# Token-major weight chunks of 512 columns in the mixers, the mLSTM gate taken before its transposes, four heads rotated at a time

## The chip, the cores and the metric

The kernel runs on one core of one Trainium2 chip. The metric is the device time of one execution in microseconds; lower is better. Five engines work side by side: PE (TensorE, matrix products), ACT (ScalarE), DVE (VectorE), POOL (GpSimd, hardly used here) and SP, which issues the transfers from memory. Each runs its own queue in order and waits for the others on semaphores.

## The reference

256 tokens of width 1024 pass through two blocks, all in float32. The change touches the two mixers of the first block: an mLSTM, and a causal attention with shared keys and values.

```python
def mlstm_mixer(x, norm_g, w_in, b_gates, h_norm_g, w_out):
    u = rmsnorm(x, norm_g) @ w_in
    q, k, v, o, gi, gf = jnp.split(u, M_SPLITS, axis=-1)   # 4 heads: q, k of 128, v, o of 256 each
    ...
    h = mlstm_chunkwise(q, k, v, i_pre, f_pre)
    h = rmsnorm(h, h_norm_g.reshape(M_HEADS, M_DV)).reshape(b_, s_, M_HEADS * M_DV)
    h = h * jax.nn.sigmoid(o.astype(jnp.float32))
    return h.astype(x.dtype) @ w_out

def shared_kv(x, norm_g, w_kv, k_norm_g, cos, sin):
    kv = rmsnorm(x, norm_g) @ w_kv
    k, v = jnp.split(kv, 2, axis=-1)                       # 8 heads of 128
    k = apply_partial_rope(rmsnorm(k.reshape(b_, s_, A_HEADS, A_DH), k_norm_g), cos, sin)
    ...

def moba_mixer(x, norm_g, w_q, q_norm_g, w_o, kb, vb, kmean, cos, sin):
    q = (rmsnorm(x, norm_g) @ w_q).reshape(b_, s_, A_HEADS, A_DH)
    q = apply_partial_rope(rmsnorm(q, q_norm_g), cos, sin) * (A_DH ** -0.5)
    ...                                                    # 256 tokens: causal softmax(q k) v
    return o @ w_o
```

After each mixer stands a convolutional feed-forward (width 2816), then the second block: two layers with a 31-tap convolution branch, an attention over the 64 best keys, and a gated output projection.

## The kernel before

Every large product is made exact enough in float32 by a split: `split_w` and `split_x` cut an operand into a high and a low part of 12 significant bits each (ACT copies the high part, DVE subtracts to get the low one), and `mm3` (lines 569 to 571) issues three matmuls, high*high, high*low, low*high. A matmul has 128 rows of contraction, 128 stationary columns and up to 512 moving columns.

**Two orientations.** `gemm_fm` (and `gemm_pair`, two of them into one PSUM bank) has the weights stationary and the 256 tokens moving, so features come out on partitions. `gemm_tm` has 128 tokens stationary and the weights moving, so a half of the tokens comes out on partitions, as wide as the weight chunk. Of the mixers' projections, before the change, `a_w_v`, `w_k`, `b_w_q` and `w_v` are token-major from chunks of 256 columns, two halves of the tokens in one bank; `a_w_o` is feature-major. All have eight contraction blocks, so a chunk of 256 costs 2 x 8 x 3 = 48 matmuls of 256 moving columns.

**mLSTM.** The gates' sums run through a small chain: a transpose of `a_s` to four rows, a copy and a running maximum on DVE (`scan`, line 477), a transpose back, then the masks E. Behind the heads' outputs `hn` (token-major) come the four `a_w_o` chunks: a `gemm_pair`, four transposes of `hn` into `tp`, then for each 128 features `so = product * r` (DVE), tanh (ACT), `y = (so + 1) * tp` (DVE), and the split of `y` with the norm's gain into `ys`, on which `proj_res("a_w_out")` works.

**Attention.** `qk_heads` works through four chunks of two heads: products for both halves of the tokens, squares with sums on ACT, the norm's factor, then for each half of the tokens two scalings (line 453) and four rotations (`tt`, line 448) on DVE, then the transposes and a copy per head on ACT.

**Memory.** Pages of on-chip memory: 24 pages "R" of 1024 columns for split parts (a weight part `w` takes a page, a token part `r` a quarter) and 25 pages "F" for raw weights and other blocks; 8 PSUM banks.

**Order.** Nothing of the engines' order is written by hand. `Program.add` records every instruction with an assumed duration; `Program.order` then plays them through and gives each engine at each moment the first recorded instruction whose operands and buffers are ready by those durations. For a matmul of a split product the assumed duration is `max(n, 256) / 2.4 + 3` ns. SP's transfers are ordered in the same way.

Late in each layer of the second block, `tap_sums` (line 1237) writes sums that go to a scratch tensor `zscr` in memory (line 1242) and come back shifted by four transfers (line 1244); the product `mm(mp, ones[0:124, :], zm[0:124, :])` waits for them on PE's queue.

Of the kernel before, what the change touches and what calls it, by code (L numbers as in the profile page):

```python
# [41 lines left out]
for _n, _c in CONSTS:  # L42
# [11 lines left out]
# buffers: name -> (page, part of a page, columns)  # L54
POOLS = {
    "w": ("R", 4, 1024),
    "r": ("R", 1, 256),
# [3 lines left out]
    "c": ("F", 2, 384),  # L61
    "s": ("s", 4, 16),
# [73 lines left out]

class Op:
# [3 lines left out]
class Program:  # L141
    """Records the kernel's instructions in order, then fixes the order in which each engine issues its own:
    the first in the program among those whose operands and buffers are ready."""
# [39 lines left out]
    @staticmethod  # L183
    def spread(ops, p0, p1):
        """Gives ops the priorities of the program's positions p0..p1."""
        for i, op in enumerate(ops):
            op.prio = p0 + (p1 - p0) * (i + 0.5) / len(ops)

    def order(self, slots):
        """slots: page name -> list of tiles. Returns the ops in the planned order, with table loads."""  # L190
# [85 lines left out]
        while left:  # L276
# [43 lines left out]
            for b in op.new:  # L320
# [7 lines left out]
                o = o * 256 if size < 4 else 0  # L328
# [53 lines left out]
def build(ctx, tc, a):  # L382
# [57 lines left out]
    # has the activation table ready for what comes after x  # L440
# [78 lines left out]
    hold = [None]  # L519

    def split_w(raw, n):
        hi, lo = new("w", n), new("w", n)
        op = act(hi, raw, AF.Copy)
        if hold[0]:
            pg.after(op, hold[0])
        tt(lo, raw, hi.f32, ALU.subtract)
        return hi, lo

    class Chunk:
        """k blocks k0..k1 of a chunk of weights; split, or as it is (native) for a float32 product; cuts: in pieces."""  # L530

        def __init__(self, dram, kc, mc, k0=0, native=False, cuts=None):
            self.mc, self.kp, self.k0 = mc, 1024 // mc, k0
            self.parts = []
            for k in range(k0, kc, self.kp):
                n = min(self.kp, kc - k) * mc
                raw = new("raw", n)
                if cuts:
                    hi, lo = new("w", n), new("w", n)
                    for c in cut(cuts, n):  # L540
                        load(raw[:, c], dram[:, k * mc + c.start:k * mc + c.stop])
                        act(hi[:, c], raw[:, c], AF.Copy)
# [4 lines left out]
                self.parts.append((raw, None) if native else split_w(raw, n))

        def at(self, k, c0, c1):
            hi, lo = self.parts[(k - self.k0) // self.kp]  # L550
            o = ((k - self.k0) % self.kp) * self.mc
            return hi[:, o + c0:o + c1], lo and lo[:, o + c0:o + c1]

    def split_x(src):
        hi, lo = new("r"), new("r")
        act(hi, src, AF.Copy)
        tt(lo, src, hi.f32, ALU.subtract)
        return hi, lo

    # a product of split operands: high*high + high*low + low*high  # L560
    def mm3(out, lhs, rhs, start, stop, check=True):
        (lh, ll), (rh, rl) = lhs, rhs[:2]
        if ll is None:
            return mm(out, lh, rhs[2], start, stop, check=check)
# [8 lines left out]
        pg.add("PE", 3 * (max(rh.n, 256) / 2.4 + 3), emit, [lh, ll, rh, rl], [out])  # L573
# [894 lines left out]
```

## Time and profile before

| | |
|---|---|
| median of 3 runs | 874.43 us (873.71, 874.43, 876.65) |
| profiled execution, first to last instruction (its span) | 873.5 us |
| PE busy | 859.4 us, 98% |
| DVE busy | 731.6 us, 84% |
| ACT busy | 559.4 us, 64% |
| transfers, share of 16 DMA engines | 56.8% |
| mean granted TensorE clock | 0.995 |

The rows below come from the one profiled execution; its own time is not listed apart from its span, which is 0.9 us under the median. Times in a timeline are microseconds from the span's start; means of one instruction are in ns. Matmuls overlap, so a matmul's own duration says little: what one costs is the distance from its start to the next one's. A float32 matmul that is not split leaves two records in the trace, a transpose one.

### The profile page before, as it was taken

What the parts mean: (1) busy time and instruction counts of PE and PEld (TensorE: products, weight loads), DVE (VectorE), ACT (ScalarE), POOL (GpSimd) and SP (SyncE); (2) the same over time, 40 slices, a digit from 0 to 9 for tenths busy, and PEclk for the clock granted to TensorE, in tenths of its full rate; (3) what the DMA queues carried; (4) which work ended last, traced back from release to release, by engine and by line L of the source; (5) the groups of instructions that cost most, each with busy time, mean ns of one, the idle gap of its engine ahead of it and who ended that gap; (6) DMA issues with size and microseconds to landing.
All of it is one profiled execution on the core that took longest, in us unless ns stands there. A gap on an engine that the chain in (4) does not pass through costs nothing.

```text
span 873.5 us, 16714 instructions
## 1 busy us (share of the span) xinstructions
PE 859.4 (98%) x6270; PEld 804.2 (92%) x6270; DVE 731.6 (84%) x1677; ACT 559.4 (64%) x1170; POOL 0.2 (0%) x4
## 2 busy tenths in 40 slices
PE   8999999999999999999999999999999999998997
PEld 8999999999999999999989999998998858997866
DVE  6757899899977699987899986675799898798895
ACT  6846577545555496874776546556953797952883
POOL 0000000000000000000000000000000000000000
PEclk9999999999999999999999999999999999999999
DMA  8987766989865354478369985642340177440101
GB/s 317 408 307 228 257 201 200 322 293 319 295 219 179 111 192 134 138 252 301 121 204 355 349 282 175 192 122 86 123 143 13 27 237 302 134 125 13 58 16 49
DMA packets 50409, 170.33 MB, mean 195 GB/s; under 512 B 5860, under 2 KB 8428, under 8 KB 50328
## 3 DMA queue, kind: packets, MB, share of 16 engines
q1 hardware_dynamic: 50184, 169.26, 56.8%
q8 instruction: 49, 0.80, 0.4%
q14 instruction: 32, 0.26, 0.1%
q10 hardware_dynamic: 144, 0.00, 0.0%
HBM read 167.88 MB, written 1.37 MB: 194 GB/s over the span
## 4 chain that ended last, share of the span: by engine, by line
PE 95%; DMA 2%; ACT 1%; DVE 1%; SPq 0%; issue 0%; DVEq 0%; ACTq 0%
PE ps L569 26%; PE ps L570 26%; PE ps L571 26%; PE ps L422 14%; PE ps L426 2%; DMA F<-zscr 1%; PE ps L580 1%; ACT F L435 1%; DMA F<-in_a_w_v_dram 1%; DVE F L453 0%; DMA zscr<-F 0%; ACT R L435 0%; DVE R L448 0%; SPq L1244 0%; PE ps L1237 0%
## 5 line engine op out<-in xcount | busy, mean ns | idle before, releaser
L569 PE MATMUL ps<-R,R 128*128 128x256 f32 (+3 forms) x1788 | 531.8, 297 | 1.3 <-ACT R L435 1.2
L570 PE MATMUL ps<-R,R 128*128 128x256 f32 (+3 forms) x1788 | 522.8, 292 | 0.5 <-DVE R L448 0.5
L571 PE MATMUL ps<-R,R 128*128 128x256 f32 (+3 forms) x1788 | 522.5, 292 | 0.0
L448 DVE TENSOR_TENSOR R<-F,R 128x1024 fp32r<-128x1024 f32 (+4 forms) x339 | 324.3, 983 | 42.0 <-ACT R L435 31.3
L569 PEld LDWEIGHTS ps<-R,R 128*128 128x128 f32 x1788 | 343.5, 192 | 10.2 <-ACT R L435 2.3
L570 PEld LDWEIGHTS ps<-R,R 128*128 128x128 f32 x1788 | 343.7, 192 | 6.8 <-DVE R L448 1.2
L571 PEld LDWEIGHTS ps<-R,R 128*128 128x128 f32 x1788 | 343.4, 192 | 5.7 <-DVE R L448 0.5
L435 ACT ACTIVATE R<-F 128x1024 fp32r<-128x1024 f32 (+4 forms) x339 | 283.1, 864 | 30.6 <-DVE F L448 24.0
L422 PE MATMUL ps<-F,F 128*128 128x256 f32 (+6 forms) x568 | 128.9, 378 | 0.9 <-ACT F L435 0.8
L435 ACT ACTIVATE F<-ps 128x256 f32<-128x256 f32 (+3 forms) x197 | 70.6, 389 | 78.3 <-PE ps L571 37.7
L422 PEld LDWEIGHTS ps<-F,F 128*128 128x128 f32 (+2 forms) x568 | 89.9, 190 | 19.6 <-issue 8.9
L435 ACT ACTIVATE F<-ps,par 128x256 f32<-128x256 f32 (+1 forms) x84 | 42.3, 552 | 93.7 <-PE ps L571 93.3
L453 DVE SCALAR_TENSOR_TENSOR F<-ps,par,F 128x255 f32<-128x255 f32 (+1 forms) x160 | 66.0, 475 | 30.7 <-ACT F L435 30.7
L453 DVE SCALAR_TENSOR_TENSOR F<-F,par,F 128x256 f32<-128x256 f32 (+11 forms) x146 | 66.5, 463 | 1.2 <-ACT F L435 1.2
L435 ACT ACTIVATE F<-F 128x256 f32<-128x256 f32 (+2 forms) x120 | 46.7, 413 | 29.7 <-DVE F L453 17.8
L453 DVE SCALAR_TENSOR_TENSOR F<-F,F 128x1024 f32<-128x1024 f32 x48 | 58.0, 1217 | 0.0
L453 DVE SCALAR_TENSOR_TENSOR F<-F,par 128x255 f32<-128x255 f32 (+14 forms) x126 | 57.8, 460 | 0.0
L448 DVE TENSOR_TENSOR F<-ps,F 128x256 f32<-128x256 f32 (+2 forms) x80 | 32.8, 439 | 21.6 <-PE ps L571 16.2
L435 ACT ACTIVATE F<-F,s 128x128 f32<-128x128 f32 (+1 forms) x80 | 33.3, 445 | 4.9 <-DVE s L474 3.8
L435 ACT ACTIVATE R<-F,par 128x256 fp32r<-128x256 f32 x32 | 14.3, 505 | 28.9 <-DVE F L448 28.9
L1364 ACT ACT_TABLE_LOAD x23 | 29.5, 1283 | 0.4
L426 PE MATMUL ps<-con,F 128*128 128x128 f32 (+2 forms) x158 | 29.4, 271 | 0.1
(96 smaller groups left out, 370.9 us busy)
## 6 DMA issues: line engine op xcount, KB each, us to landing
F<-in_f_w_up_dram SPq DMA_DIRECT2D x88, 512.0 KB, 5.3
F<-in_w_ada_dram SPq DMA_DIRECT2D x48, 512.0 KB, 5.1
F<-in_f_w_down_dram SPq DMA_DIRECT2D x44, 512.0 KB, 5.9
F<-in_w_u_dram SPq DMA_DIRECT2D x16, 512.0 KB, 5.3
F<-in_w_out_dram SPq DMA_DIRECT2D x16, 512.0 KB, 3.8
F<-in_a_w_o_dram SPq DMA_DIRECT2D x8, 512.0 KB, 10.2
F<-in_a_w_out_dram SPq DMA_DIRECT2D x8, 512.0 KB, 10.2
F<-in_w_k_dram SPq DMA_DIRECT2D x8, 512.0 KB, 5.3
```

The lines of the kernel that those rows point to most:

```text
L422: pg.add("PE", dur, lambda: nc.tensor.matmul(g(out), g(lhsT), g(rhs), start=start, stop=stop, skip_group_check=not check), [lhsT, rhs], [out])
L426: pg.add("PE", 110.0, lambda: nc.tensor.transpose(g(out), g(x), g(idn)), [x, idn], [out])
L435: nc.scalar.activation(g(out), g(x), func, bias=g(bias), scale=g(scale), **kw)
L448: return pg.add("DVE", ddur(n or x.n), lambda: nc.vector.tensor_tensor(g(out), g(x), g(y), op), [x, y], [out])
L453: nc.vector.scalar_tensor_tensor(g(out), g(x), g(s), g(y), op0, op1, **kw)
L569: nc.tensor.matmul(o, g(lh), g(rh), start=start, stop=False, **kw)
L570: nc.tensor.matmul(o, g(lh), g(rl), start=False, stop=False, **kw)
L571: nc.tensor.matmul(o, g(ll), g(rh), start=False, stop=stop, **kw)
L580: nc.tensor.matmul(g(out[e * 64:e * 64 + 64, c]), g(v[s][e]), g(p[e][:, r]), start=s == 0, stop=s == 1, skip_group_check=True)
L1364: nc.scalar.preload_act_table_set(TABLE[op[1]])
```

## The change

Five edits go together.

1. The chunks of `a_w_v` (heads 1 and 2 in one, head 3 alone), `a_w_o`, `w_k`, `b_w_q` and `w_v` have 512 columns; each half of the tokens goes to a PSUM bank of its own.
2. `a_w_o` becomes token-major. ACT takes the tanh straight from PSUM with the norm's factor as its scale (512 columns at once), DVE multiplies with `hn`, and the transposes come behind that; the split of `ys` reads the transposed product from PSUM.
3. `qk_heads` norms, rotates and transposes four heads at a time, one half of the tokens after the other.
4. A split operand is one buffer, high part beside low part (`Sp`): 12 pages "R" of 2048 columns, a weight part takes a page, a token part a quarter.
5. The planner assumes 13.5 ns (`PASS`) beside the columns for a matmul of a split product, not 3.

```diff
 PAGES = {
-    "R": (1024, F32R, 24),
+    "R": (2048, F32R, 12),
...
 POOLS = {
-    "w": ("R", 4, 1024),
-    "r": ("R", 1, 256),
+    "w": ("R", 4, 2048),
+    "r": ("R", 1, 512),
...
+    "h": ("F", 2, 512),
...
+PASS = 13.5
...
     def split_w(raw, n):
-        hi, lo = new("w", n), new("w", n)
-        op = act(hi, raw, AF.Copy)
+        w = Sp(new("w"), 0, n)
+        op = act(w.hi, raw, AF.Copy)
         if hold[0]:
             pg.after(op, hold[0])
-        tt(lo, raw, hi.f32, ALU.subtract)
-        return hi, lo
+        tt(w.lo, raw, w.hi.f32, ALU.subtract)
+        return w
...
-        pg.add("PE", 3 * (max(rh.n, 256) / 2.4 + 3), emit, [lh, ll, rh, rl], [out])
+        pg.add("PE", 3 * (max(n, 256) / 2.4 + PASS), emit, [lh, ll, rb], [out])
...
-        if h:
-            ch = Chunk(a["a_w_v"][h - 1], 8, 256)
-            ps = psum()
+        if h in (1, 3):
+            ch = Chunk(a["a_w_v"][0], 8, 512) if h == 1 else Chunk(a["a_w_v3"][0], 8, 256)
+            n = 512 if h == 1 else 256
+            ps = [psum()[:, 0:n] for _ in range(2)]
             for t in range(2):
-                gemm_tm(half(ps, t), [ch.at(k, 0, 256) for k in range(8)], xs, t)
+                gemm_tm(ps[t], [ch.at(k, 0, n) for k in range(8)], xs, t)
...
+    rch = small(2)
+    ts(rch, rc, 0.5, None, ALU.mult)
     ys = []
-    for j in range(4):
-        ps = gemm_pair(Chunk(a["a_w_o"][j], 8, 256), xs)
-        tp = psum()
-        for b in range(2):
-            for t in range(2):
-                tr(tp[:, b * S + t * 128:b * S + t * 128 + 128], hn[j * 2 + t][:, b * 128:b * 128 + 128], ident)
-        for b in range(2):
-            m = 2 * j + b
-            so, y = blk(), blk()
-            tt(so, half(ps, b), r, ALU.mult)
-            first_s = act(so, so, AF.Tanh, scale=0.5)
-            stt(y, so, 1.0, half(tp, b), ALU.add, ALU.mult)
-            yh, yl = new("r"), new("r")
-            act(yh, y, AF.Copy, scale=ghalf[:, m:m + 1])
-            stt(yl, y, ghalf[:, m:m + 1], yh.f32, ALU.mult, ALU.subtract)
-            ys.append((yh, yl))
+    for j in range(2):
+        ch, yt = Chunk(a["a_w_o"][j], 8, 512), []
+        for t in range(2):
+            ps, so = psum(), new("h")
+            gemm_tm(ps, [ch.at(k, 0, 512) for k in range(8)], xs, t)
+            first_s = act(so, ps, AF.Tanh, scale=rch[:, t:t + 1])
+            for i in range(2):
+                y = blk()
+                stt(y, so[:, i * 256:i * 256 + 256], 1.0, hn[(2 * j + i) * 2 + t], ALU.add, ALU.mult)
+                yt.append(y)
+        for i in range(2):
+            tp = psum()
+            for b in range(2):
+                for t in range(2):
+                    tr(tp[:, b * S + t * 128:b * S + t * 128 + 128], yt[t * 2 + i][:, b * 128:b * 128 + 128], ident)
+            for b in range(2):
+                m, yp = 4 * j + 2 * i + b, Sp(new("r"))
+                act(yp.hi, half(tp, b), AF.Copy, scale=ghalf[:, m:m + 1])
+                stt(yp.lo, half(tp, b), ghalf[:, m:m + 1], yp.hi.f32, ALU.mult, ALU.subtract)
+                ys.append(yp)
...
     def qk_heads(dram, xs, gain):
-        for j in range(4):
-            ch = Chunk(a[dram][j], 8, 256)
...
+        for j in range(2):
+            ch = Chunk(a[dram][j], 8, 512)
             hs = []
             for t in range(2):
-                o, t2 = blk(), blk()[:, 0:64]
-                for i in range(2):
+                ps, qq, ms = psum(), small(4), small(4)
+                gemm_tm(ps, [ch.at(k, 0, 512) for k in range(8)], xs, t)
+                for i in range(4):
+                    act(blk()[:, 0:128], ps[:, i * 128:i * 128 + 128], AF.Square, accum_out=qq[:, i:i + 1])
+                ts(ms, qq, 1.0 / 128, e2[:, t:t + 1], ALU.mult, ALU.add)
+                rr = rstd_cols(ms, 4)
+                o, t2 = new("h"), blk()[:, 0:128]
+                for i in range(4):
...
             for i in range(2):
-                tp, o = psum(), blk()
-                for t in range(2):
-                    tr(tp[:, t * 128:t * 128 + 128], hs[t][:, i * 128:i * 128 + 128], ident)
-                act(o, tp[:, 0:256], AF.Copy)
-                yield o
+                tp, o = psum(), new("h")
+                for e in range(2):
+                    for t in range(2):
+                        tr(tp[:, e * S + t * 128:e * S + t * 128 + 128], hs[t][:, (2 * i + e) * 128:(2 * i + e) * 128 + 128], ident)
+                act(o, tp, AF.Copy)
+                yield half(o, 0)
+                yield half(o, 1)
...
     vt = []
-    for j in range(4):
-        ch = Chunk(a["w_v"][j], 8, 256)
-        ps = psum()
-        vt.append([blk(), blk()])
+    for j in range(2):
+        ch = Chunk(a["w_v"][j], 8, 512)
+        vt.append([new("h"), new("h")])
         for t in range(2):
-            gemm_tm(half(ps, t), [ch.at(k, 0, 256) for k in range(8)], xkv, t)
-        for t in range(2):
-            act(vt[j][t], half(ps, t), AF.Copy, scale=rc[:, t:t + 1])
+            ps = psum()
+            gemm_tm(ps, [ch.at(k, 0, 512) for k in range(8)], xkv, t)
+            act(vt[j][t], ps, AF.Copy, scale=rc[:, t:t + 1])
```

The layout of the weights in memory follows (`_chunks(..., 8, 512)`). In all, PE's program has 5324 rows in place of 5756.

The planner's order moves with it. **First place:** PE at the mLSTM gates' running maximum. The first row is the transpose that the maximum starts from, the last two are the transpose of its result and the first mask product; between them stand matmuls of an `a_w_v` product (R buffers). Before, 27 of them (three shown):

```order
L426 MATMUL ps_158<-con,s_122 4x128 x2
L569 MATMUL ps_154<-R_67,R_63 128x256
L570 MATMUL ps_154<-R_69,R_63 128x256
L571 MATMUL ps_154<-R_67,R_63 128x256
...
L426 MATMUL ps_152<-con,F_87 128x4 x2
L422 MATMUL ps_155<-F_87,F_106 128x256
```

Now nine of 512 columns, and one float32 product ahead of them:

```order
L464 MATMUL ps_142<-con,s_111 4x128 x2
L460 MATMUL ps_141<-F_88,F_89 128x128
L607 MATMUL ps_146<-R_65,R_63 128x512
L608 MATMUL ps_146<-R_65,R_63 128x512
L609 MATMUL ps_146<-R_65,R_63 128x512
...
L464 MATMUL ps_140<-con,F_75 128x4 x2
L460 MATMUL ps_143<-F_75,F_94 128x256
```

By columns, PE has two thirds of the work there that it had while DVE works on the maximum.

**Second place:** the end of the mLSTM gate. Before, on PE, the last `a_w_o` product, the transposes of `hn` (ready long since), and the first `a_w_out` product:

```order
L571 MATMUL ps_158<-R_70,R_77 128x256
L426 MATMUL ps_156<-con,F_87 128x128 x4
L569 MATMUL ps_152<-R_80,R_76 128x256
L570 MATMUL ps_152<-R_80,R_76 128x256
L571 MATMUL ps_152<-R_80,R_79 128x256
```

Now, after the last `a_w_o` matmul, two transposes of the first half of the tokens, 21 matmuls of `a_w_out` (two shown), six transposes of which four wait for the second half's gate, and 15 more matmuls of `a_w_out` before the next that needs the new `ys`:

```order
L609 MATMUL ps_142<-R_69,R_66 128x512
L464 MATMUL ps_144<-con,F_75 128x128
L464 MATMUL ps_140<-con,F_75 128x128
L607 MATMUL ps_143<-R_74,R_70 128x256
...
L609 MATMUL ps_145<-R_74,R_72 128x256
L464 MATMUL ps_144<-con,F_81 128x128
L464 MATMUL ps_144<-con,F_75 128x128
L464 MATMUL ps_144<-con,F_81 128x128
L464 MATMUL ps_140<-con,F_77 128x128
```

And DVE there now: four splits of `a_w_out`, the two gate products, two products for the later `mods` (the 1024-column rows into `mod`), and then the low parts of `ys`:

```order
L486 TENSOR_TENSOR R_63<-F_78,R_63 128x1024
L486 TENSOR_TENSOR R_67<-F_82,R_67 128x1024
L491 SCALAR_TENSOR_TENSOR F_81<-F_81 128x256
L491 SCALAR_TENSOR_TENSOR F_77<-F_81,F_77 128x256
L491 SCALAR_TENSOR_TENSOR F_94,mod_155<-F_94,F_84 128x1024
L491 SCALAR_TENSOR_TENSOR F_91,mod_155<-F_91,F_84 128x1024
L491 SCALAR_TENSOR_TENSOR R_66<-ps_144,s_100,R_66 128x256 x2
L491 SCALAR_TENSOR_TENSOR R_66<-ps_140,s_100,R_66 128x256 x2
```

**Third place:** PE around `zscr` in the first layer of the second block, which the diff does not touch. Before, 69 matmuls (two shown) stand between `tap_sums` and the product that waits for `zscr`:

```order
L1237 MATMUL ps_154<-F_104,par 32x256
L1237 MATMUL ps_154<-F_106,par 32x256 x2
L569 MATMUL ps_153<-R_78,R_65 128x256
...
L571 MATMUL ps_155<-R_66,R_76 128x256
L422 MATMUL ps_152<-F_101,con 128x256
```

Now 63:

```order
L1277 MATMUL ps_146<-F_89,par 32x256
L1277 MATMUL ps_146<-F_78,par 32x256 x2
L607 MATMUL ps_142<-R_73,R_74 128x256
...
L609 MATMUL ps_140<-R_63,R_68 128x256
L460 MATMUL ps_141<-F_91,con 128x256
```

Six matmuls of 256 columns fewer stand there. In the second layer it is 66 before and now.

## Rows read from the trace of the kernel before

**Rows 1.** The page's busy times: engine, busy us, share of the span, instructions.

```profile
PE 859.4 (98%) x6270; PEld 804.2 (92%) x6270; DVE 731.6 (84%) x1677; ACT 559.4 (64%) x1170; POOL 0.2 (0%) x4
```

**Rows 2.** The page's chain that ended last, its shares of the span by engine.

```profile
PE 95%; DMA 2%; ACT 1%; DVE 1%; SPq 0%; issue 0%; DVEq 0%; ACTq 0%
```

**Rows 3.** Waits of PE's queue: us in total, times, longest.

```profile
PE ps L422 <- DMA F<-zscr: 4.4, 2, 3.1
PE ps L569 <- ACT R L435: 1.2, 2, 0.7
```

**Rows 4.** Groups of PE's instructions by form: count, then busy us, mean ns.

```profile
L569 PE MATMUL ps<-R,R 128*128 128x256 f32 x1624 | 468.5, 289 | 0.0
L569 PE MATMUL ps<-R,R 128*128 128x512 f32 x116 | 45.5, 393 | 0.0
```

**Rows 5.** Timeline of PE in the first feed-forward: start us, duration us.

```profile
299.30 0.28 PE L569 MATMUL ps<-R,R 128*128 128x256 f32 x1
...
312.62 0.28 PE L569 MATMUL ps<-R,R 128*128 128x256 f32 x1
```

**Rows 6.** Timeline of PE in the second feed-forward's last products.

```profile
593.20 0.40 PE L569 MATMUL ps<-R,R 128*128 128x512 f32 x1
...
605.22 0.39 PE L571 MATMUL ps<-R,R 128*128 128x512 f32 x1
```

**Rows 7.** A stretch: us, PE busy (instructions), PEclk granted, DMA share, GB/s.

```profile
49.30:52.50 3.20, 3.20 (x16) 0.50 1.03 410
```

**Rows 8.** Stretches, all engines: us, busy of PE, PEld, DVE, ACT, POOL.

```profile
65.00:90.00 25.00, 25.00 (x197) 24.50 (x196) 19.95 (x56) 16.20 (x41) 0.00 (x0) 1.00 0.68 221
330.00:420.00 90.00, 90.00 (x734) 89.11 (x733) 79.83 (x255) 59.65 (x165) 0.00 (x0) 1.00 0.61 207
```

**Rows 9.** Timeline of all engines at the running maximum of the mLSTM gates.

```profile
42.40 0.38 PE L426 MATMUL ps<-con,s 128*4 128x128 f32 x2
...
42.82 0.41 DVE L468 COPY F<-ps 4x256 f32<-4x256 f32 x1
...
43.16 1.20 DVE L448 TENSOR_TENSOR R<-F,R 128x1024 fp32r<-128x1024 f32 x1
...
44.29 0.67 DVE L477 TENSOR_TENSOR_SCAN F<-F 4x256 f32<-4x256 f32 x1
...
45.94 0.28 PE L426 MATMUL ps<-con,F 4*128 4x4 f32 x2
```

**Rows 10.** Groups of ACT's instructions by form: count, busy us, mean ns.

```profile
L435 ACT ACTIVATE R<-F 128x1024 fp32r<-128x1024 f32 x230 | 237.6, 1050 | 0.8 <-PE ps L570 0.5 <-PE ps L571 0.3
...
L435 ACT ACTIVATE F<-ps 128x512 f32<-128x512 f32 x8 | 4.8, 598 | 1.2 <-PE ps L422 0.9 <-PE ps L426 0.3
```

**Rows 11.** Groups of DVE's instructions by form.

```profile
L448 DVE TENSOR_TENSOR R<-F,R 128x1024 fp32r<-128x1024 f32 x230 | 276.2, 1218 | 22.1 <-ACT R L435 13.6 <-issue 7.8 <-PE ps L571 0.3
...
L448 DVE TENSOR_TENSOR F<-F,F 128x64 f32<-128x64 f32 x30 | 6.6, 220 | 0.1
...
L453 DVE SCALAR_TENSOR_TENSOR F<-F,ps 128x256 f32<-128x256 f32 x16 | 6.2, 410 | 0.0
...
L453 DVE SCALAR_TENSOR_TENSOR R<-F,s,R 128x256 fp32r<-128x256 f32 x8 | 3.6, 482 | 1.7 <-ACT R L435 1.7
```

**Rows 12.** Timeline of PE around `zscr`, first and second layer.

```profile
657.27 0.67 PE L1237 MATMUL ps<-F,par 128*32 128x256 f32 x8
667.76 0.67 PE L422 MATMUL ps<-F,con 124*128 124x256 f32 x2 [1.35 <-DMA F<-zscr]
...
786.28 0.67 PE L1237 MATMUL ps<-F,par 128*32 128x256 f32 x8
798.12 0.67 PE L422 MATMUL ps<-F,con 124*128 124x256 f32 x2 [3.05 <-DMA F<-zscr]
```

**Rows 13.** Transfers by tensor: count, KB each, us from issue to landing.

```profile
F<-in_f_w_up_dram SPq DMA_DIRECT2D x88, 512.0 KB, 5.3
```

More of the change, by code (lines that the diff above doesn't have):

```diff
@@ L134, in get, with __init__, __getitem__, hi @@
         return self.fn(a) if self.fn else a
+class Sp:
+    def __init__(self, v, o=0, n=None, x=None):
+        self.v, self.o, self.h, self.x = v, o, v.buf.cols // 2, x
+        self.n = self.h if n is None else n
+    def __getitem__(self, c):
+        c0, c1, _ = c.indices(self.n)
+        return Sp(self.v, self.o + c0, c1 - c0, self.x and self.x[:, c])
+    @property
+    def hi(self):
+        return self.v[:, self.o:self.o + self.n]
+    @property
+    def lo(self):
+        return self.v[:, self.h + self.o:self.h + self.o + self.n]
+    @property
+    def both(self):
+        o, n, h = self.o, self.n, self.h
+        return V(self.v.buf, fn=lambda a: a.rearrange("p (e c) -> p e c", e=2)[:, :, o:o + n], iv=[(o, o + n), (h + o, h + o + n)])
+class Native:
+    def __init__(self, x):
+        self.x = x
+    def __getitem__(self, c):
+        return Native(self.x[:, c])
 class Op:
@@ L327, in order @@
                 b.slot = (page, i, o, size)
-                o = o * 256 if size < 4 else 0
+                o = o * (PAGES[page][0] // 4)
                 b.ap = slots[page][i][:, o:o + cols]
@@ L585, in mm_tm @@
     def mm_tm(out, x, w, t, start, stop):
-        c = slice(t * 128, t * 128 + 128)
-        if w[1] is None:
-            mm(out, x[2][:, c], w[0], start, stop, check=False)
-        else:
-            mm3(out, (x[0][:, c], x[1][:, c]), w, start, stop, check=False)
+        mm3(out, x[t * 128:t * 128 + 128], w, start, stop, check=False)
     def gemm_fm(out, ws, xs):
@@ L1059, in __init__ @@
             self.l, self.h, self.r = l, h, [None, None]
-            self.hi, self.lo, self.x = ([new(p) for _ in range(2)] for p in ("w", "w", "raw"))
+            self.hl, self.x = ([new(p) for _ in range(2)] for p in ("w", "raw"))
             self.xs = []
@@ L1150, in dsa_layer @@
         lat = [psum() for _ in range(2)]
-        cq = [(new("r"), new("r")) for _ in range(2)]
+        cq = [Sp(new("r")) for _ in range(2)]
         kix, kvT, ws = blk(), blk(), small(16)
@@ L1305, in dsa_layer @@
             tt(t, uv[:, 0:S], gates[hp], ALU.mult)
-            mix[4 + hp] = (None, None, t) if "oa" in NATIVE else split_x(t)
+            mix[4 + hp] = Native(t) if "oa" in NATIVE else split_x(t)
         hd.load_gain()
@@ L1317, in dsa_layer @@
             act(t2, t, AF.Silu, bias=pcols("conv_ln_b_2", l * 4 + j), scale=pcols("conv_ln_g_2", l * 4 + j))
-            ln.append((None, None, t2) if "pw" in NATIVE else split_x(t2))
+            ln.append(Native(t2) if "pw" in NATIVE else split_x(t2))
         preload("E", t2)
@@ L1421, in _layout @@
     out["a_w_k"] = _chunks(w[:, 512:1024], 8, 256)
-    out["a_w_v"] = _chunks(w[:, 1280:2048], 8, 256)
-    out["a_w_o"] = _chunks(w[:, 2048:3072], 8, 256)
+    out["a_w_v"] = _chunks(w[:, 1280:1792], 8, 512)
+    out["a_w_v3"] = _chunks(w[:, 1792:2048], 8, 256)
+    out["a_w_o"] = _chunks(w[:, 2048:3072], 8, 512)
     out["a_w_out"] = _chunks(f["a_w_out"][0], 8, 256)
@@ L1431, in _layout @@
     out["f_w_down"] = np.concatenate(downs)
-    out["w_k"] = _chunks(f["w_kv"][:, :D], 8, 256)
-    out["w_v"] = _chunks(f["w_kv"][:, D:], 8, 256)
-    out["b_w_q"] = _chunks(f["b_w_q"][0], 8, 256)
+    out["w_k"] = _chunks(f["w_kv"][:, :D], 8, 512)
+    out["w_v"] = _chunks(f["w_kv"][:, D:], 8, 512)
+    out["b_w_q"] = _chunks(f["b_w_q"][0], 8, 512)
     out["b_w_o"] = _chunks(f["b_w_o"][0], 8, 256)
```

87 lines of the change are left out of this document (39 added, 48 removed).

## Prediction

> **What bounds the kernel.** I read the busy times first: PE is busy for 859.4 of 873.5 us and DVE for 731.6 [rows 1]. A busy PE need not be the bound, so the chain of waits comes next: 95% of it lies on PE, 2% on transfers [rows 2]. Then what PE's queue waits for: a scratch transfer, 4.4 us in two waits, and little else; no wait for weight parts passes 0.7 us [rows 3]. In two stretches of the mixers PE is busy throughout, with DVE at 19.95 of 25 and 79.83 of 90 us [rows 8]. So the time is PE's stream of matmuls, laid end to end, and a change pays by what it takes out of that stream, less what it makes PE wait.
>
> What one matmul costs is read from start to start. In the first feed-forward 111 starts of 256-column split matmuls lie between 299.30 and 312.62: 13.32 / 111 = 120.0 ns [rows 5]. In the second one's last products 53 of 512 columns lie between 593.20 and 605.22: 12.02 / 53 = 226.8 ns [rows 6]. The means of the groups, 289 and 393 ns [rows 4], contain the overlap and aren't used. Two matmuls of 256 columns cost 240.0 ns, one of 512 costs 226.8: a merged pair gives back 13.2 ns.
>
> **Part by part.**
>
> *Wider chunks.* A chunk of 256 costs 48 matmuls. `w_k`, `b_w_q`, `w_v` and `a_w_o` had four each, 768 in all, and now have 384 of twice the width: 384 fewer. Heads 1 and 2 of `a_w_v` had 96 and now 48. Together 432 fewer, which is also 5756 - 5324 rows. All of them stood on PE's path: 432 x 13.2 = 5.7 us less. Bounds: nothing, if a merged matmul ran as long as its two; 5.7 us, if rows 6 hold here. I take 5.7: rows 6 are of the same form, tokens stationary, weights moving.
>
> Here a rule of the Trainium skill stands against the row (TensorE: Matmul & The Clock Gate, Back-to-back issue gap): a warm matmul costs its columns at 2.4 GHz and about 2.5 ns. By that a merged pair would give 2.5 ns, an estimate of 1.1 us for 432. The rows show more, 120.0 and 226.8 ns, so the rows decide.
>
> *The running maximum (first place).* PE's transpose starts at 42.40; DVE's copy, a weight split of 1.20 us and the maximum follow, which ends at 44.29 + 0.67 = 44.96; PE went on to the transpose of the result at 45.94, held by its 27 matmuls [rows 9]. With a hand-over of 0.2 us (an estimate, on the safe side of the 0.04 us between the transposes' end and the copy) PE could go on at 45.16, that is 2.76 us after the start. Now it has two transposes and a float32 product, about 0.44 us by the distances of their columns, and 9 x 226.8 = 2.04 us: 2.48 us. So about 0.3 us of wait are new. Bounds: nothing, if the split doesn't stand before the maximum; 1.5 us, if it starts a whole split later. I take 0.3.
>
> *The gate (second place).* Eight DVE products with `r` go, about 0.4 us each by the nearest row [rows 11], and tanh is taken of 512 columns at once, about 0.6 us by ACT's row of that width [rows 10]; neither is on PE's path now, so I cost the saving at nothing. What is new: PE's transposes wait for the gate. After the last `a_w_o` matmul come tanh 0.6 and two gate products of 0.41 [rows 10, 11], with three hand-overs of 0.2: 2.0 us. PE has two transposes and 21 x 0.120 = 2.5 us of `a_w_out` before it needs them. The cover is there by 0.6 us. Then DVE issues two 1024-column products, about 1.22 us each by the split's row [rows 11], ahead of the low parts of `ys`: the first low part is ready some 2.0 + 2.4 + 0.5 = 4.9 us after the last `a_w_o` matmul. PE reaches it after 2.7 us, six transposes (0.6) and 15 + 3 matmuls (2.2): 5.5 us. I cost this at nothing; if a 1024-column operand came late, the wait would be up to 1.2 us, one such product. Queued behind it on DVE are the other low parts, and PE waits for each.
>
> *Four heads at a time.* The rotations are 32 DVE instructions fewer, at 220 ns for the larger kind [rows 11], but twice as wide; transposes are copied 512 columns at once. DVE has 10 us to spare in this stretch [rows 8], so this saves nothing, and no transfer is added: the bytes are the same. Cover for the longer group is `w_v`: 96 matmuls of 512 columns, 21.8 us on PE.
>
> *Pages.* No instruction is added or dropped. What could be lost is that a split needs one whole page of 12, where it needed two of 24 at two moments; see the rivals.
>
> *The planner's 13.5 ns.* 256 / 2.4 + 13.5 = 120.2 ns is what rows 5 show; so the planned moments come nearer to the chip's. It moves instructions everywhere. Where PE waited longest I looked: in the first layer `tap_sums` started at 657.27 and the waiting product at 667.76, with 69 matmuls between; in the second 786.28, 798.12 and 66 [rows 12]. The transfers set 10.5 and 11.8 us. Now the first has 63: 6 x 0.120 = 0.7 us more wait (the third place); the second has 66 still, nothing. Bounds: 0 to 0.7 us in the first; 1 us to either side in the second, whose scratch transfers took 1.35 us longer than the first's.
>
> *Sum,* against the profiled execution: 873.5 - 5.7 + 0.3 + 0.7 = 868.8. The median of the runs stands 0.9 us over that span, so I forecast **869.7**.
>
> *The clock.* From 49.30 to 52.50 PE had the lower clock: 16 matmuls where 27 go [rows 7], which cost some 1.6 us. Just before stood the mask products with 4 rows of contraction. They stay as they are, so I keep this cost; without it the time is 868.1, with a second such stretch 871.3.
>
> **The rivals.**
>
> *(a) A merged matmul gives less.* If what a matmul costs beside its columns went with the weights that it loads and the data that it moves, a merged one would run like two, and only the new waits would remain: 873.5 + 1.0 + 0.9 = 875.4. By the page named above it would be an estimate of 1.1 us below that. Rows 5 and 6 speak against it. Chance 0.04.
>
> *(b) Larger pieces leave bubbles.* The trace for it: ACT and DVE aren't full [rows 8], and the covers at the gate are 0.6 us. If the gate gives 1.2 us and each of the four groups of heads 0.5, the time is 869.7 + 3.2 = 872.9, no change that can be told. Against it: before, PE waited for ACT 1.2 us in all [rows 3]. Chance 0.17. The Trainium skill has the rule that speaks for it (Perfetto Trace Analysis, Optimizing Scalar/DVE Operations): where Scalar and DVE aren't full but hold up other engines, smaller instructions may let work end sooner. The trace doesn't show such a hold-up before.
>
> *(c) Slower: pages of doubled size run out.* A token part in a page keeps 2048 columns from a weight part, where it kept 1024. If a page came free late at one stage's edge, the split would come late, its raw buffer stay taken, and the next chunk's transfer wait: 5.3 us to land [rows 13], a split of 1.05 on ACT and 1.22 on DVE [rows 10, 11], 7.6 us on PE. One such case decides: 869.7 + 7.6 = 877.3. Against it: in the planned orders, with buffer numbers, the tightest weight page has 11 products of three matmuls between the last reader of its old content and the first of the new before, and 12 now, at least 4.3 us, and a split takes 2.3. Chance 0.05.
>
> That the change doesn't do what it says is excluded by the 432 rows.
>
> **How the numbers follow.** The forecast has 0.74, with (a), (b) and (c) as above. A measurement of this kernel can tell about 0.3%, 2.6 us: faster means under 871.8, slower over 877.1. Nearly all of the forecast's case lies under 871.8, some of its upper end (a second clock stretch, the second layer's transfers) not; a little of (b) stays under: faster 0.75, same 0.20, slower 0.05. The range: down, no clock stretch (-1.6), the two new waits absent (-1.0) and half a microsecond of old waits gone, 869.7 - 3.1 = 866.6; up, to rival (b) and a little past it, 873.3. It leaves out (a), (c) and the far end of (b).
>
> **What would show it.** PE: 432 matmuls fewer, 512-column starts 227 ns apart in the mixers, the first feed-forward starting 1.5 us earlier or more. The wait for `zscr` in the first layer near 2.1 us, in the second near 3. A wait of some 0.3 us at the maximum. None over 0.5 us at PE's transposes of the gate. Wrong would be: starts near 240 ns (a); waits on ACT or DVE of over 2 us in all within the mixers (b); a wait for an R buffer of several microseconds (c).

## The result, and the profile after

| | before | after |
|---|---|---|
| median of the runs beside each other | 874.1 us (873.71 to 876.65) | 882.18 us (880.96 to 882.74) |
| ratio | 1 | 1.0085, 95% interval 1.0065 to 1.0105 |
| profiled execution, span | 873.5 us | 881.0 us |

By the ratio the change made the kernel slower by 0.85%, which is 7.4 us of 874.1 (the two medians are 8.1 us apart), where 4.7 us less were forecast. The page's busy times after, the two lines that answer to [rows 1, 2], tell nothing of it at first: PE is as busy as before. The chain does: PE's share of it has fallen from 95% to 86%, and DVE and ACT have come in.

```profile
PE 860.7 (98%) x5838; PEld 784.6 (89%) x5838; DVE 723.9 (82%) x1630; ACT 557.8 (63%) x1154; POOL 0.2 (0%) x4
...
PE 86%; DVE 7%; ACT 3%; DMA 2%; issue 1%; SPq 0%; DVEq 0%; ACTq 0%
```

**Where it happened.** Four landmarks on PE, each from the timeline of either kernel, and the end cut the span into stages. The two that [rows 12] show of before are the starts of `tap_sums`; the other two are the first product of 456 columns of each layer in the second block. Of before:

```profile
610.65 0.36 PE L569 MATMUL ps<-R,R 128*128 128x456 f32 x1
...
739.62 0.47 PE L569 MATMUL ps<-R,R 128*128 128x456 f32 x1 [0.49 <-ACT R L435]
```

The same four after:

```profile
605.79 0.36 PE L607 MATMUL ps<-R,R 128*128 128x456 f32 x1
...
651.64 0.66 PE L1277 MATMUL ps<-F,par 128*32 128x256 f32 x6
...
738.10 0.48 PE L607 MATMUL ps<-R,R 128*128 128x456 f32 x1 [0.45 <-ACT R L473]
...
790.38 0.66 PE L1277 MATMUL ps<-F,par 128*32 128x256 f32 x6
```

| landmark | before | after | after - before |
|---|---|---|---|
| first 456-column product, layer 0 | 610.65 | 605.79 | -4.9 |
| `tap_sums`, layer 0 | 657.27 | 651.64 | -5.6 |
| first 456-column product, layer 1 | 739.62 | 738.10 | -1.5 |
| `tap_sums`, layer 1 | 786.28 | 790.38 | +4.1 |
| end | 873.5 | 881.0 | +7.5 |

Up to the end of the first block, whose mixers the change rewrites, 4.9 us are gained. Some 0.8 of them are chance: before, a stretch at the lower clock (8.2 to 11.7, granted 0.50) lay in the start, and the last product of 264 columns stands at 14.77 before and 13.97 after. The second block lost 12.4. The diff changes the buffers of its split operands, but no instruction: PE has 1569 records there in either trace.

**The mixers after.** From 315.15 to 321.06 stand 26 distances between products of 512 columns: 5.91 / 26 = 227.3 ns, near the 226.8 of [rows 6].

```profile
315.15 0.39 PE L607 MATMUL ps<-R,R 128*128 128x512 f32 x1
...
321.06 0.39 PE L609 MATMUL ps<-R,R 128*128 128x512 f32 x1
```

**What PE waits for after** (us in total, times, longest), to be read against [rows 3]:

```profile
PE ps L464 <- DVE F L497: 3.1, 1, 3.1
PE ps L1277 <- DVE F L491: 2.4, 2, 1.5
PE ps L460 <- issue: 2.3, 1, 2.3
PE ps L460 <- DMA F<-zscr: 2.1, 1, 2.1
...
PE ps L607 <- ACT R L473: 0.7, 2, 0.5
PE ps L460 <- DVE F L497: 0.7, 1, 0.7
PE ps L464 <- DVE F L515: 0.4, 1, 0.4
```

Two rows answer to the scratch transfers: 2.1 us in layer 0, and 2.3 in layer 1 (which the profile puts under "issue"). Together they are what they were, 4.4. The row of L515 is the running maximum. New are two kinds: 3.1 and 0.7 us at the layer boundary (L464 waits for DVE's L497), and 2.4 us in which `tap_sums` waits for DVE.

**The layer boundary.** Between the two layers ACT has two things to do: the squares of the second token half's output (`F<-ps 128x256`, four of them, then two small steps of the norm), from which the next layer's second half follows, and the first half's features (`F<-ps,mod` and `R<-F 128x256`). ACT before, the second half's last squares and then the features:

```profile
736.38 0.38 ACT L435 ACTIVATE F<-ps 128x256 f32<-128x256 f32 x1
...
737.02 0.38 ACT L435 ACTIVATE F<-ps 128x256 f32<-128x256 f32 x1 [0.18 <-PE ps L571]
...
737.40 0.38 ACT L435 ACTIVATE F<-ps 128x256 f32<-128x256 f32 x1
...
738.22 0.20 ACT L435 ACTIVATE s<-s 128x1 f32<-128x1 f32 x1
738.33 0.79 ACT L435 ACTIVATE F<-ps,mod 128x128 f32<-128x128 f32 x2
```

ACT after: two squares, a weight split, all features, and only then the other two squares, though the last of PE's products for them started at 735.47:

```profile
735.31 0.37 ACT L473 ACTIVATE F<-ps 128x256 f32<-128x256 f32 x1
...
735.67 1.05 ACT L473 ACTIVATE R<-F 128x1024 fp32r<-128x1024 f32 x1
736.79 0.81 ACT L473 ACTIVATE F<-ps,mod 128x128 f32<-128x128 f32 x2
...
741.06 0.42 ACT L473 ACTIVATE R<-F 128x256 fp32r<-128x256 f32 x1
741.38 0.37 ACT L473 ACTIVATE F<-ps 128x256 f32<-128x256 f32 x1
...
741.74 0.37 ACT L473 ACTIVATE F<-ps 128x256 f32<-128x256 f32 x1
```

So the second half's norm is ready at 742.8, not 738.4. PE's cover (the work it has while it would otherwise wait) is the first half's 24 products of 456 columns, 5 us. Before, PE did 21 of them and then, at 744.35, its products for the second half's features, which the norm lets start:

```profile
744.35 1.95 PE L422 MATMUL ps<-F,F 128*128 128x128 f32 x16
```

Now all 24 end at 743.4 and the products for the second half's features cannot start. What PE stands for until 746.49 is the transposes of the first half's own latents: their scaling (L497) is in DVE's queue behind the second half's update and squares, which start at 742.80. The second half's feature products follow at 747.82, after the wait of 0.7.

```profile
745.95 0.48 DVE L497 TENSOR_SCALAR F<-ps,s 128x256 f32<-128x256 f32 x1
...
746.49 0.63 PE L464 MATMUL ps<-con,F 128*128 128x128 f32 x3 [3.11 <-DVE F L497]
```

**The tap sums.** `tap_sums` needs four `u2` products of DVE. Before, the last one started at 785.57, in time:

```profile
785.57 0.41 DVE L453 SCALAR_TENSOR_TENSOR F<-F,ps 128x256 f32<-128x256 f32 x1
```

After, DVE has eleven products of the 31 taps (255 columns and fewer) ahead of it, and PE waits 1.53 us:

```profile
787.79 4.40 DVE L491 SCALAR_TENSOR_TENSOR F<-F,par 128x255 f32<-128x255 f32 x11
792.10 0.42 DVE L491 SCALAR_TENSOR_TENSOR F<-F,ps 128x256 f32<-128x256 f32 x1
...
792.57 0.65 PE L1277 MATMUL ps<-F,par 128*32 128x256 f32 x2 [1.53 <-DVE F L491]
```

**The clock.** Three stretches stand at the lower clock (1.2 GHz, granted 0.50) that were not there before: one behind layer 0's scratch wait, one from 746.8 to 753.5 behind the boundary's wait, one behind layer 1's scratch wait. A window in each, of all engines (columns as in [rows 8]):

```profile
664.80:668.20 3.40, 3.40 (x19) 3.40 (x18) 3.40 (x11) 0.00 (x0) 0.00 (x0) 0.51 0.02 5
749.60:753.00 3.40, 3.40 (x15) 3.17 (x14) 2.85 (x4) 3.01 (x8) 0.00 (x0) 0.50 0.79 247
804.80:808.20 3.40, 3.40 (x17) 3.31 (x16) 3.40 (x10) 0.51 (x2) 0.00 (x0) 0.51 0.02 5
```

PE works at half speed there: 3.3, 6.7 and 3.3 us at the lower clock cost at most half of it, 6.7 us. With the new waits, 3.8 at the boundary and 2.4 at the tap sums, that is 12.9 us as an upper end, against 12.4 lost.

### The profile page after: what moved, and what is told of

Its sections match the earlier page's. It is cut to its first block, busy times and chain, and to the rows that moved or that the text cites. A ratio compares the mean times of both kernels' runs of the same rounds, so it can differ in the third digit from the quotient of the medians.

```text
span 881.0 us, 15806 instructions
## 1 busy us (share of the span) xinstructions
PE 860.7 (98%) x5838; PEld 784.6 (89%) x5838; DVE 723.9 (82%) x1630; ACT 557.8 (63%) x1154; POOL 0.2 (0%) x4
## 4 chain that ended last, share of the span: by engine, by line
PE 86%; DVE 7%; ACT 3%; DMA 2%; issue 1%; SPq 0%; DVEq 0%; ACTq 0%
PE ps L608 24%; PE ps L607 24%; PE ps L609 24%; PE ps L460 12%; DVE F L491 3%; PE ps L464 2%; DVE R L486 2%; ACT F L473 1%; DMA F<-zscr 1%; DVE F L521 1%; DVE s L518 1%; ACT R L473 1%; PE ps L618 1%; DMA F<-in_a_w_v_dram 1%; DMA zscr<-F 0%
## 5 line engine op out<-in xcount | busy, mean ns | idle before, releaser
L607 PE MATMUL ps<-R,R 128*128 128x256 f32 (+2 forms) x1644 | 506.4, 308 | 0.7 <-ACT R L473 0.7
L608 PE MATMUL ps<-R,R 128*128 128x256 f32 (+2 forms) x1644 | 498.3, 303 | 1.1 <-DVE R L486 0.9
L609 PE MATMUL ps<-R,R 128*128 128x256 f32 (+2 forms) x1644 | 497.8, 303 | 0.0
L607 PEld LDWEIGHTS ps<-R,R 128*128 128x128 f32 x1644 | 315.9, 192 | 15.7 <-ACT R L473 2.0
L608 PEld LDWEIGHTS ps<-R,R 128*128 128x128 f32 x1644 | 316.1, 192 | 13.0 <-DVE R L486 2.6
L609 PEld LDWEIGHTS ps<-R,R 128*128 128x128 f32 x1644 | 315.6, 192 | 11.5 <-DVE R L486 0.2
L460 PE MATMUL ps<-F,F 128*128 128x256 f32 (+5 forms) x566 | 129.1, 383 | 1.1 <-DVE F L497 0.7
L473 ACT ACTIVATE F<-ps 128x256 f32<-128x256 f32 (+5 forms) x189 | 69.9, 397 | 70.5 <-PE ps L609 43.0
L491 DVE SCALAR_TENSOR_TENSOR F<-ps,par,F 128x255 f32<-128x255 f32 (+1 forms) x160 | 66.2, 476 | 49.6 <-ACT F L473 49.2
L491 DVE SCALAR_TENSOR_TENSOR F<-F,par 128x255 f32<-128x255 f32 (+29 forms) x188 | 78.3, 462 | 0.1
L491 DVE SCALAR_TENSOR_TENSOR F<-F,F 128x1024 f32<-128x1024 f32 (+1 forms) x54 | 59.8, 1130 | 6.7 <-ACT F L473 5.4
L473 ACT ACTIVATE F<-F 128x256 f32<-128x256 f32 (+2 forms) x112 | 43.8, 412 | 26.7 <-DVE F L491 16.0
L486 DVE TENSOR_TENSOR F<-ps,F 128x256 f32<-128x256 f32 (+2 forms) x72 | 29.7, 442 | 20.8 <-PE ps L609 18.7
L491 DVE SCALAR_TENSOR_TENSOR F<-F,par,F 128x256 f32<-128x256 f32 (+16 forms) x84 | 38.1, 466 | 0.4 <-ACT F L473 0.4
L486 DVE TENSOR_TENSOR F<-F,F 128x256 f32<-128x256 f32 (+2 forms) x83 | 29.4, 361 | 1.1 <-ACT F L473 0.4
L464 PE MATMUL ps<-con,F 128*128 128x128 f32 (+2 forms) x158 | 26.8, 273 | 3.5 <-DVE F L497 3.1
```

Of the source, the lines that this page charges most:

```text
L460: pg.add("PE", dur, lambda: nc.tensor.matmul(g(out), g(lhsT), g(rhs), start=start, stop=stop, skip_group_check=not check), [lhsT, rhs], [out])
L464: pg.add("PE", 110.0, lambda: nc.tensor.transpose(g(out), g(x), g(idn)), [x, idn], [out])
L473: nc.scalar.activation(g(out), g(x), func, bias=g(bias), scale=g(scale), **kw)
L486: return pg.add("DVE", ddur(n or x.n), lambda: nc.vector.tensor_tensor(g(out), g(x), g(y), op), [x, y], [out])
L491: nc.vector.scalar_tensor_tensor(g(out), g(x), g(s), g(y), op0, op1, **kw)
L607: nc.tensor.matmul(o, g(lh), g(rh), start=start, stop=False, **kw)
```

## The experiments

**Theory A:** the mixers gained what was forecast, and what is lost comes from the planner's assumed duration of a matmul, 13.5 ns in place of 3: PE's products end later in the plan, so other instructions come first on ACT and DVE. **Theory B:** the larger pages and pieces leave fewer moments to place a split. Ratios below are to runs of the kernel before on the same chip, with 95% intervals.

**1. The changed kernel planned as before.**

```diff
-PASS = 13.5
+PASS = 3.0
```

> The changed kernel whole, but the planner assumes 3 ns beside the columns again. Theory A (the mixers gained what was forecast, and the 13 us lost lie in the second block, where the new assumed duration turned the order): the gain of the mixers stays and the loss goes, 874.1 - 5 = 869 us (867 to 872), the two waits at the layer boundary (3.1 us at the latent's transposes, 0.7 at the products behind) gone. Theory B (the loss comes from the larger pages and pieces, which leave fewer moments to place a split): the time stays near 882 us (880 to 884).

Measured: 873.86 us, ratio 0.9979 (0.9963 to 0.9995). One number brings back 0.0106, some 9 us; B falls. But 869 was expected. The first 456-column product starts at 605.44, so the mixers' gain is there; what is left stands in the waits:

```profile
PE ps L460 <- DMA F<-zscr: 3.4, 2, 1.7
PE ps L464 <- DVE F L497: 2.3, 1, 2.3
```

The boundary still costs 2.3 us and a stretch at the lower clock (741.8 to 748.6). All four squares now come first, but the two small steps of the norm behind them still stand after the features (at 737.58 and 737.89, the features from 732.99). At the same 3 ns the kernel before has no such wait [rows 3]; whether the new pages or the mixers' other durations bring it, no run tells.

**2. The kernel before with the new number.**

```diff
-        pg.add("PE", 3 * (max(rh.n, 256) / 2.4 + 3), emit, [lh, ll, rh, rl], [out])
+        pg.add("PE", 3 * (max(rh.n, 256) / 2.4 + 13.5), emit, [lh, ll, rh, rl], [out])
```

> The kernel before, its code untouched but for the planner's assumed duration: 13.5 ns in place of 3. Theory A: its second block loses too, since ACT's queue at the layer boundary then puts the second pair of squares of the second token half behind the ten features' activations, as in the changed kernel; 874.1 + 7 = 881 us or more (878 to 888). Theory B: no change, 874 us within 1.

Measured: 889.4 us, ratio 1.0145 (1.0118 to 1.0171). Without any edit to the mixers, the same rows appear, the squares behind the features among them:

```profile
PE ps L422 <- DMA F<-zscr: 5.5, 2, 3.2
PE ps L426 <- DVE F L459: 2.9, 1, 2.9
PE ps L1237 <- DVE F L453: 2.3, 2, 1.2
```

```profile
748.31 0.37 ACT L435 ACTIVATE F<-ps 128x256 f32<-128x256 f32 x1
```

That row is the third of the second half's four squares; the first half's features run from 743.72 to 748.31.

So 13.5 ns by itself costs 12.7 us, and the rest of the change is worth 1.0145 - 1.0085 = 0.006, 5 us.

**3. Only the boundary's order mended**, with 13.5 ns kept. `early` holds the squares of the second half and its norm's steps, `f0` the place of the first feature:

```diff
+            if t and not last:
+                for op in early + pg.ops[s0:]:
+                    op.prio = f0 - 0.5
```

> The changed kernel; only at the layer boundary the planner ranks the squares of the second token half's output and the four small steps of its norm ahead of the first half's features. Theory A: PE's wait of 3.1 us at the latent's transposes, the 0.7 us behind it and the lower clock that follows (some 1.7 us) go, 882.2 - 5.5 = 876.7 us (875 to 879); the waits around the scratch tensor stay. Rival: another instruction is late next (the update of h on DVE, or a weight split), the wait moves on, and the time stays within 1 us of 882.2.

Measured: 875.9 us, ratio 1.0002 (0.9987 to 1.0018), 0.0083 under the changed kernel, some 7 us, a little more than expected. ACT now has the squares at 735.00 and 735.37, ahead of the features at 735.73, and PE's longest wait at the boundary is 1.4 us, for a feature that these squares hold up. The lower clock at the boundary is gone.

```profile
PE ps L460 <- DMA F<-zscr: 4.7, 2, 2.4
PE ps L1277 <- DVE F L491: 2.5, 2, 1.6
PE ps L607 <- ACT R L473: 1.4, 1, 1.4
```

**4. The merging undone alone.** The planned order is kept; each 512-column product is issued as two pieces. The mixers' projections come out with other values in this kernel; it is read for PE's time alone.

```diff
+            for p in range(pieces):
+                c = slice(p * n // pieces, (p + 1) * n // pieces)
+                o = g(out[:, c])
+                nc.tensor.matmul(o, g(lh), g(rh)[:, c], start=start, stop=False, **kw)
...
```

> The changed kernel with its planned order kept; only PE issues each 512-column product of the mixers as two pieces of 256, which are 432 matmuls more. Forecast's price: 432 x 13.2 ns = 5.7 us more, all before the first feed-forward, 882.2 + 5.7 = 887.9 us (886.5 to 889). If merging gives nothing: 882.2 us. By 2.5 ns for each matmul: 883.3 us.

Measured: 886.66 us, ratio 1.0114 (1.0086 to 1.0143). The medians put 4.5 us on it, the ratios 2.5, and the two intervals overlap: the time alone does not settle the price. The landmark, of one profiled execution each, does better: the first 456-column product starts at 610.21 in place of 605.79, 4.4 us later, 10 ns for each of 432. That excludes both a gain of nothing and the 1.1 us of 2.5 ns each; 5.7 is a little too much.

**5 and 6. Both orders mended.** Run 5 has 3 ns and the edit of run 3; run 6 also lets the planner put more work ahead of the product that waits for `zscr`:

```diff
-ZDUR, ZTAIL = 480.0, 4000.0
+ZDUR, ZTAIL = 480.0, 7500.0
```

> The changed kernel with both edits: the planner assumes 3 ns, and the second half's squares and norm are ranked ahead of the first half's features. Theory A: with 3 ns alone a wait of 2.3 us at the latent's transposes, 0.4 behind it and a stretch at the lower clock (some 1.5 us) were left at the layer boundary; they go now, so about 4 us under the run with 3 ns alone: 0.9979 x 874.1 - 4 = 868.3 us, a ratio of 0.993 (0.991 to 0.996). Rival: the wait moves to the next late instruction, the ratio stays at 0.998.

> As the run before, and the planner assumes 7.5 us in place of 4 for the shifted transfers back from the scratch tensor, so that it puts 87 and 92 matmuls ahead of the product that waits for them (70 and 82 without). Theory A: the two waits of 3.4 us in all and the lower clock after them go, 2 to 4 us less: a ratio near 0.990 (0.987 to 0.993). Rival: the product's result is then late for the 31-tap sums on DVE, or the matmuls that were put ahead are missing later; no gain, a ratio of 0.993 or more.

Measured: 868.27 us, ratio 0.9917 (0.9899 to 0.9935), and 866.18 us, 0.9889 (0.9870 to 0.9908). Both as expected. In run 6 no wait for `zscr` is left, and behind the start PE waits nowhere longer than 0.9 us.

**7 and 8. Other numbers**, nothing else changed: `PASS = 8.0` and `PASS = -4.0`.

> The changed kernel, the planner's assumed duration at 8 ns, between 3 and 13.5. Theory A in its stronger form (the shorter PE's planned time, the earlier ACT and DVE are made to serve it, a margin that the chip needs): between the two, a ratio of 1.000 to 1.006 (874 to 879 us), with 64 matmuls ahead of the scratch product as at 13.5. Rival (the order is chaotic, and 13.5 ns was only an unlucky value): anywhere, under 0.998 or over 1.008 as likely as between.

> The changed kernel, the planner's assumed duration at -4 ns: PE planned faster than it can be. Theory A in its stronger form: not above the run at 3 ns, a ratio of 0.990 to 0.998 (865 to 872 us), with 79 and 73 matmuls ahead of the scratch products. Rival (13.5 ns was an unlucky value, or PE now outruns its weights in the plan and waits for splits elsewhere): 0.998 or more.

Measured: at 8 ns 876.48 us, ratio 1.002 (1.0006 to 1.0034), between 3 and 13.5 as a margin would have it. At -4 ns 887.49 us, 1.0129 (1.0109 to 1.0149): the stronger form of A, by which a shorter assumed time only helps, is wrong there. The first block loses: the first 456-column product starts at 616.76, 11.3 us later than at 3 ns. Two of its waits, the second followed by the lower clock from 139.8 to 143.2 (granted 0.51):

```profile
PE ps L464 <- DVE F L486: 3.0, 1, 3.0
PE ps L609 <- DVE R L486: 2.1, 1, 2.1
```

The first is PE at the transposes of four rotated heads. DVE put weight splits between the small steps of the heads' norm. That it did so because the plan wanted the weights sooner than PE did is argued, not shown:

```profile
350.28 0.15 DVE L486 TENSOR_TENSOR s<-s,s 128x4 f32<-128x4 f32 x1
350.35 1.22 DVE L486 TENSOR_TENSOR R<-F,R 128x1024 fp32r<-128x1024 f32 x1
351.49 0.15 DVE L486 TENSOR_TENSOR s<-s,s 128x4 f32<-128x4 f32 x1
351.56 1.22 DVE L486 TENSOR_TENSOR R<-F,R 128x1024 fp32r<-128x1024 f32 x1
```

The waits over the four numbers, in us:

| assumed, ns | -4 | 3 | 8 | 13.5 |
|---|---|---|---|---|
| ratio | 1.0129 | 0.9979 | 1.0020 | 1.0085 |
| first 456-column product at | 616.76 | 605.44 | 605.42 | 605.79 |
| wait at the boundary's transposes | 3.1 | 2.3 | 2.3 | 3.1 |
| `tap_sums` waits for DVE | none | 0.4 | 0.9 | 2.4 |
| waits for `zscr` | 1.5 | 3.4 | 4.0 | 4.4 |

The tap sums and the scratch product follow the number step by step; the boundary does not. Four values do not exclude that the order is chaotic in the number and 13.5 an unlucky one; what is shown is which waits each order made.

**9 and 12. The kernel before with the two edits of order**, its 3 ns kept. The trace read here is run 12's.

> The kernel before, with the two edits of order alone (squares ranked first; 7.5 us assumed for the transfers back from the scratch tensor, which puts 87 and 89 matmuls ahead of the waiting product in place of 70 and 67). Theory A: its two scratch waits of 4.4 us go, its layer boundary has little to gain: 874.1 - 4 = 870 us, a ratio of 0.995 (0.992 to 0.998), so that on equal orders the mixers' edits are worth about 5 us (0.9889 against 0.995). Rival (the good ratio of 0.9889 is mostly the order's, the mixers' edits give nothing by themselves): a ratio of 0.991 or less.

> The same kernel as in the run of the kernel before with the two edits of order, for its profile: a ratio near 0.994, no wait over 1 us for the scratch transfers, the first product of 456 columns near 612 us as before.

Measured: 870.09 us, ratio 0.9942 (0.9924 to 0.9961), and 871.0 us, 0.9943 (0.9924 to 0.9962). No wait for `zscr` is left. The landmark of run 12 stands at 608.19, not near 612 (before it was 610.65): this execution had full clock from 8.3 to 11.7 and from 49.2 to 52.6. Against run 6, with the same edits and the same number, the mixers' edits are worth 0.9943 - 0.9889 = 0.0054, 4.7 us; the two intervals, each some 0.002 to either side, do not meet.

**10 and 11. The two edits of order with 6 and with 13.5 ns.**

> The changed kernel with the two edits of order and 6 ns in the planner in place of 3. If what 13.5 ns cost came through the layer boundary and the scratch products alone, which the two edits now settle by themselves, 6 ns does as well as 3: a ratio of 0.987 to 0.991. Rival (the margin matters in many more places): 0.992 or more.

> The changed kernel as it is (13.5 ns) with the two edits of order; 87 matmuls now stand ahead of each scratch product. If the layer boundary and the scratch products were all that 13.5 ns cost, the ratio is that of 3 and 6 ns with the same edits, 0.989 (0.987 to 0.991). If the wait of the tap sums for DVE (2.5 us in two places at 13.5 ns) and what follows it count beside them, 0.992 to 0.996.

Measured: at 6 ns 864.98 us, ratio 0.9887 (0.9870 to 0.9905), the fastest with run 6; at 13.5 ns 871.1 us, 0.9950 (0.9935 to 0.9965). So 3 and 6 are equal once the two places are mended, and 13.5 keeps a loss of 0.006 of its own. The waits of run 11 show the tap sums in it, and behind the longer of them PE had the lower clock:

```profile
PE ps L1277 <- DVE F L491: 2.5, 2, 1.6
```

```profile
785.12 0.65 PE L1277 MATMUL ps<-F,par 128*32 128x256 f32 x2 [1.65 <-DVE F L491]
```

```profile
786.80:790.20 3.40, 3.40 (x19) 3.40 (x18) 3.40 (x10) 2.27 (x4) 0.00 (x0) 0.50 0.14 43
```

The rest of that loss is not placed: this execution also had the lower clock from 46.1 to 52.9 (granted 0.50), where the changed kernel's had one half as long.

In run 10 PE does not wait at the tap sums, behind the start its longest wait is 0.9 us, and there is no idle time from 736 to 756 and from 780 to 810:

```profile
736.00:756.00 20.00, 20.00 (x151) 19.12 (x150) 14.69 (x21) 19.08 (x53) 0.00 (x0) 1.00 0.34 107
780.00:810.00 30.00, 30.00 (x205) 27.20 (x205) 28.60 (x88) 15.40 (x35) 0.00 (x0) 1.00 0.07 23
```

## Why the prediction was wrong, step by step

*Wider chunks, -5.7.* The mechanism was right, the size a little off. The products of 512 columns stand 227.3 ns apart in the mixers, near [rows 6]. But the landmark behind the first block moved by 4.9 - 0.8 = 4.1 us, 4.5 without the new wait at the maximum; run 4 gives 4.4, and the comparison on equal orders 4.7. The term was some 1 us too large, and the traces show most of it: rows 5 and 6 stand in the feed-forwards. Over the mixers' own split products (14 to 140 and 312 to 420 us; only distances under 140 ns for 256 columns and under 260 for 512), the mean from start to start is 119.8 and 119.7 ns of 256 columns before, 227.6 and 228.6 ns of 512 after. By these a pair gives back 12.0 ns in the mLSTM and 10.8 in the attention, an estimate of 4.8 us for the 432. Rival (a) is out. With it goes the estimate of 1.1 us by the Trainium skill's gap of 2.5 ns (TensorE: Matmul & The Clock Gate, Back-to-back issue gap): this kernel's rows have 120.0 and 226.8 ns, and the runs went with the rows.

*The running maximum, +0.3.* Right: 0.4 us, the split of 1.20 us ahead of the maximum as the order showed.

*The gate, 0.* Right: no wait of PE's transposes there appears among its waits.

*Four heads, 0, and pages, 0.* Right at this order: PE's waits for split parts on ACT are 0.7 us, before 1.2 [rows 3]. Rivals (b) and (c) did not come. Run 8 shows that the heads' long chain on DVE is a weak place all the same: 3.0 us where the splits are planned sooner.

*The planner's 13.5 ns, +0.7.* **This step failed.** It said that the planned moments come nearer to the chip's, that instructions move everywhere, and then it looked only where PE had waited longest, at the two scratch products. Those came out near what was written: 2.1 us in the first layer and 2.3 in the second, where 2.1 and near 3 had been said, so together they added nothing. But a new order makes new waits where there were none, and the sum had nothing for them: 3.8 us at the layer boundary, 2.4 at the tap sums, and the lower clock behind them and behind the scratch waits. Run 2 puts the number's whole price at 12.7 us in the kernel before, run 1 at some 9 us in the changed one. The step's first sentence was itself the trap: 13.5 ns does fit PE, yet the planner gives each engine the first recorded instruction that is ready by its durations and knows no urgency. With 3 ns PE's results came early in the plan, so what hangs on them (the squares, the last `u2`) was ready before the idle engine took something of lower rank. The plan's error was a margin. That this is the way it works is argued from the code; that the number does it, and that the squares' place costs 7 us, is shown by runs 1, 2 and 3.

*The clock.* The forecast kept one stretch at the lower clock and priced a second one at 1.6 us. Four came while PE had work, one of them 6.7 us long. The one that it kept does not belong to the mask products with 4 rows: run 12 has the same products and full clock there. And the profile before had a second one already, from 8.2 to 11.7, which the forecast did not read.

The rival that was missing: that the order of the second block, which the change turns without touching its instructions, loses more than the mixers gain. It could have been seen in part. The orders of ACT and DVE at the boundary were there to compare; a look at every place where PE's cover is a fixed block of matmuls (the 24 products at the boundary, the four `u2` ahead of `tap_sums`) and at what its releaser has in front of it would have found both places, if not the lower clock behind them.

## What to carry to other kernels

When a change alters a number that a scheduler plans by, cost it as a change of its own: list the places where a critical engine's cover is short, and compare what its releasers now have queued ahead. A more exact duration need not give a better order, where ready instructions are taken without regard to who waits for them. Here an assumed duration a little too short on the bounding engine (3 or 8 ns) did better than the exact one, and one far too short (-4 ns) did worse; that the first acts as a margin is argued. Mend such places by rank, not by the number: here the two edits of rank and of the scratch transfers' time were worth 0.0135 at 13.5 ns and 0.009 at 3 ns, and with them 3 and 6 ns are alike (0.9889 and 0.9887).

## What the runs showed of the hardware

A wait of PE is not always followed by the lower clock. After the changed kernel's waits of 2.1, 3.1 and 2.3 us PE got 1.2 GHz for 3.3, 6.7 and 3.3 us; before, the wait of 3.05 us in layer 1 [rows 12] was followed by full clock, as this window just behind it shows:

```profile
799.20:802.60 3.40, 3.40 (x24) 3.19 (x23) 3.40 (x11) 0.66 (x2) 0.00 (x0) 1.00 0.00 0
```

Nor must a wait be that long: run 11's wait of 1.65 us was followed by 1.2 GHz from 786.8 to 790.2.

The Trainium skill (TensorE: Matmul & The Clock Gate, Part 1, What's actually happening) calls the ramp at a kernel's start run-variable for the same kernel. The traces agree: before, PE had 1.2 GHz from 8.2 to 11.7, and in run 12, with the same instructions on PE up to there, the full clock. In sums such as the forecast's, a new wait of the sizes seen here (1.65 to 3.1 us) should therefore carry a possible 1.7 us on top, an estimate from half of 3.3, and twice that for the longer stretch.
